# Kurtosis of 1024 rows: the last stage summed on TensorE with a factor row, other piece sizes, another split of x^4

## The chip, the cores and the metric

The kernel runs on one core of one Trainium2 chip. The metric is the device time of one execution in microseconds (us). A load moves data from HBM to SBUF; TensorE (PE) multiplies matrices into PSUM; VectorE (DVE), ScalarE (ACT) and GpSimd (POOL) work on tiles; SyncE (SP) issues the transfers.

## The reference

The input is 1024 rows of 8192 float32. Each row gives one number, its excess kurtosis:

```python
mean = np.mean(x, axis=-1, keepdims=True)
std = np.std(x, axis=-1, keepdims=True)
z = (x - mean) / (std + 1e-8)
return (np.mean(z ** 4, axis=-1) - 3).astype(np.float32)
```

With p2 and p4 the sums of the squared and fourth powers of x - mean, this is n p4 / p2^2 - 3, n = 8192 (the kernel leaves out the 1e-8).

## The kernel before

The rows are worked in 18 groups. A group takes 128/k rows, cut into k segments each, so that all 128 partitions are filled. Groups 0 and 1 have k = 8 (1024 columns a partition), group 2 has k = 4 (2048), groups 3 to 17 have k = 2 (4096 columns, 2 MB). `GROUPS` lists for each group k, the pieces in which its columns are loaded, how many columns of the fourth power ScalarE takes, and who sums for the mean. `load` issues one transfer per piece on SP's queue. The tiles lie in five slots (`SLOT_OF`), and `load_next` issues a group's loads, in order, when the group that held its slot is done.

The order of the work is written out by hand in the loop `for i in range(L)` (L = 17, the last group). Step i does this:

- `mean(i)`. For the first six groups VectorE adds the halves of the tile (`added_halves`, L149) and TensorE multiplies by a block matrix (L159). For 'PE' groups TensorE transposes the tile in chunks of 128 columns, adding them all up in `tps` (`transposed_sums`, L132); VectorE adds pairs of columns into `red` (`pair_sums`, L138), and a matmul with a column of -1/n gives minus the mean in `mps` (L168). The last group is of kind 'both': transposes for all but its last 512 columns, `added_halves` for these, two matmuls (L164, L165). ScalarE copies `mps` to `nmu` (L170).
- `square(i)`: ScalarE writes (x - mean)^2 over the tile and accumulates its sum in `s2` (L176).
- `fourth_dve(i - 1, ...)`: VectorE squares the previous group's tile again from some column on, and accumulates in `qd` (L188). Then `load_next(i - 1)`.
- a piece of the last stage of an earlier batch, if one is due in this step (`STEPS`).
- `fourth_act(i, ...)`: ScalarE does the same for the first columns, accumulating in `qa` (L183).

The groups are put into four batches for the last stage: groups 0 and 1, group 2, groups 3 to 12, groups 13 to 17. `finish(b)` is a generator in three parts, and `STEPS` says in which steps of the loop the parts of the first three batches are run: (7, 8, 9), (9, 10, 11) and (13, 14, 15). Its parts are `factor` (p2 = the segments' `s2` added up by a matmul, L204, and `fac` = -1/p2^2 by L206 and L208 on VectorE), `scaled` (`w4` = (qa + qd) times `fac`, L215 and L216) and `result` (a matmul into `pk` that adds up a row's segments and lays rows along the free axis, L226; minus 3, L228; the output transfer, L230).

The last group and the last batch are written out behind the loop. The last group's square is done in two halves of 2048 columns, the second half of the tile first, each with its own column of `s2`. VectorE does x^4 of columns 2048 to 4095 and of 1664 to 2047 (384 columns), and ScalarE of the first 1664. ScalarE multiplies its own sum by the factor (`wa`, L290), VectorE its own (L292), and two matmuls add `wa` and `w4` into one `pk`.

Of the kernel before, what the change touches and what calls it, by code (L numbers as in the profile page):

```python
# [7 lines left out]
f32 = mybir.dt.float32  # L8
bf16 = mybir.dt.bfloat16
AO = mybir.AluOpType  # L10
AF = mybir.ActivationFunctionType
P = 128
# [7 lines left out]
    (2, [4096], 1280, 'DVE'),  # L20
    (2, [4096], 768, 'DVE'),
    (2, [4096], 1536, 'DVE'),
    (2, [2304, 1792], 640, 'PE'),
    (2, [2304, 1792], 640, 'PE'),
    (2, [2304, 1792], 640, 'PE'),
    (2, [2304, 1792], 640, 'PE'),
    (2, [2304, 1792], 640, 'PE'),
    (2, [2304, 1792], 640, 'PE'),
    (2, [2304, 1792], 640, 'PE'),
    (2, [1536, 1536, 1024], 512, 'PE'),  # L30
    (2, [1536, 1536, 1024], 512, 'PE'),
    (2, [1536, 1536, 1024], 512, 'PE'),
    (2, [1536, 1536, 1024], 512, 'PE'),
    (2, [1536, 1280, 768, 512], 1664, 'both'),
]

BATCHES = [[0, 1], [2], [3, 4, 5, 6, 7, 8, 9, 10, 11, 12], [13, 14, 15, 16, 17]]
SLOT_W = 4096
SLOT_OF = [0, 1, 2, 3, 0, 1, 2, 3, 4, 0, 1, 2, 3, 4, 0, 1, 2, 3]
HALVES = 2  # L40


@with_exitstack
def kernel(
# [5 lines left out]
    nc = tc.nc  # L50
    n_rows, n_cols = x.shape
# [3 lines left out]
    L = NG - 1  # L55
    KS = [g[0] for g in GROUPS]
# [4 lines left out]
    const = ctx.enter_context(tc.tile_pool(name="const", bufs=1))  # L61
    small = ctx.enter_context(tc.tile_pool(name="small", bufs=4))
    fin = ctx.enter_context(tc.tile_pool(name="fin", bufs=4))
    psum = ctx.enter_context(tc.tile_pool(name="psum", bufs=2, space=bass.MemoryType.PSUM))
    psfin = ctx.enter_context(tc.tile_pool(name="psfin", bufs=1, space=bass.MemoryType.PSUM))
# [7 lines left out]
    blk = {}  # L73

    def block_matrix(k):
        r = P // k
        b = const.tile([P, P], f32, name=f"blk{k}")
        v = b.rearrange("p (r k) -> p r k", k=k)
        nc.gpsimd.memset(b, neg_inv_n)
        nc.gpsimd.affine_select(  # L80
            out=v, in_=v, pattern=[[-k, r], [0, k]], base=0,
            channel_multiplier=1, compare_op=AO.is_ge, fill=0.0)
        nc.gpsimd.affine_select(  # L83
            out=v, in_=v, pattern=[[k, r], [0, k]], base=k - 1,
            channel_multiplier=-1, compare_op=AO.is_ge, fill=0.0)
        blk[k] = b

    for k in dict.fromkeys(k for k in KS if k > 2):
# [4 lines left out]
        out=ident, in_=ident, pattern=[[-1, P]], base=0,  # L93
        channel_multiplier=1, compare_op=AO.is_equal, fill=0.0)
    negcol = const.tile([P, 1], f32, name="negcol")
    nc.gpsimd.memset(negcol, neg_inv_n)
    block_matrix(2)
    junk = const.tile([P, 2048], bf16, name="junk")

    where = {}
    stats = []
    for b in BATCHES:
        n = len(b) + (b[-1] == L)
        s2, qa, qd = (const.tile([P, n], f32, name=f"{t}_{b[0]}") for t in ("s2", "qa", "qd"))
        if any(GROUPS[i][2] == 0 for i in b):
            nc.gpsimd.memset(qa, 0.0)
        stats.append((s2, qa, qd))
        for j, i in enumerate(b):  # L110
            where[i] = (j, s2, qa, qd)

    slots = [xpool.tile([P, SLOT_W], f32, name=f"xt{s}") for s in sorted(set(SLOT_OF))]
    xts = {}
# [40 lines left out]
    def mean(i):  # L155
        k, pieces, _, engine = GROUPS[i]
        mps = psum.tile([P, 1], f32, name="mps")
        if engine == "DVE":
            nc.tensor.matmul(mps, lhsT=blk[k], rhs=added_halves(i, 0), start=True, stop=True)  # L159
        elif engine == "both":  # L160
            c = sum(pieces[:-1])
            tps = transposed_sums(i, c)
            part = added_halves(i, c)
            nc.tensor.matmul(mps, lhsT=pair_sums(tps), rhs=negcol, start=True, stop=False)  # L164
            nc.tensor.matmul(mps, lhsT=blk[k], rhs=part, start=False, stop=True)  # L165
        else:
            tps = transposed_sums(i, n_cols // k)
            nc.tensor.matmul(mps, lhsT=pair_sums(tps), rhs=negcol, start=True, stop=True)  # L168
        nmu = small.tile([P, 1], f32, name="nmu")
        nc.scalar.copy(nmu, mps)  # L170
        nmus[i] = nmu

    def square(i, c0=0, c1=None, extra=0):
        j, s2, qa, qd = where[i]
        t = xts[i][:, c0:c1]
        nc.scalar.activation(out=t, in_=t, func=AF.Square, bias=nmus[i],  # L176
                             accum_out=s2[:, j + extra:j + extra + 1])

    def fourth_act(i, c0, c1):
        j, s2, qa, qd = where[i]  # L180
        if c1 > c0:
            t = xts[i][:, c0:c1]
            nc.scalar.activation(out=t, in_=t, func=AF.Square, accum_out=qa[:, j:j + 1])  # L183

    def fourth_dve(i, c0, c1=None, extra=0):
        j, s2, qa, qd = where[i]
        t = xts[i][:, c0:c1]
        nc.vector.tensor_tensor_reduce(  # L188
            out=t, in0=t, in1=t, scale=1.0, scalar=0.0,
            op0=AO.mult, op1=AO.add, accum_out=qd[:, j + extra:j + extra + 1])  # L190

    def factor(b):
        s2 = stats[BATCHES.index(b)][0]
        n = len(b)
        k = KS[b[0]]
        p2 = psfin.tile([P, n], f32, name="p2")
        if b[-1] == L:
            nc.tensor.matmul(p2[:, :n - 1], lhsT=blk[k], rhs=s2[:, :n - 1], start=True, stop=True)  # L200
            nc.tensor.matmul(p2[:, n - 1:n], lhsT=blk[k], rhs=s2[:, n - 1:n], start=True, stop=False)  # L201
            nc.tensor.matmul(p2[:, n - 1:n], lhsT=blk[k], rhs=s2[:, n:n + 1], start=False, stop=True)
        else:
            nc.tensor.matmul(p2, lhsT=blk[k], rhs=s2, start=True, stop=True)  # L204
        rec = fin.tile([P, n], f32, name="rec")
        nc.vector.reciprocal(rec, p2)  # L206
        fac = fin.tile([P, n], f32, name="fac")
        nc.vector.scalar_tensor_tensor(  # L208
            out=fac, in0=rec, scalar=-1.0, in1=rec, op0=AO.mult, op1=AO.mult)
        return fac  # L210

    def scaled(b, fac, n):
        s2, qa, qd = stats[BATCHES.index(b)]
        w4 = fin.tile([P, len(b)], f32, name="w4")
        nc.vector.tensor_add(w4[:, :n], qa[:, :n], qd[:, :n])  # L215
        nc.vector.tensor_mul(w4[:, :n], w4[:, :n], fac[:, :n])  # L216
        return w4

    def result(b, terms):
        n = len(b)  # L220
        k = KS[b[0]]
        r = P // k
        sel = blk[k].rearrange("p (r k) -> p r k", k=k)[:, :, 0]
        pk = psfin.tile([n, r], f32, name="pk")
        for j, t in enumerate(terms):
            nc.tensor.matmul(pk, lhsT=t, rhs=sel, start=j == 0, stop=j == len(terms) - 1)  # L226
        kr = fin.tile([n, r], f32, name="kr")
        nc.vector.tensor_scalar_add(kr, pk, -3.0)  # L228
        dst = out[ROWS[b[0]]:ROWS[b[-1] + 1]].rearrange("(g r) -> g r", r=r)
        nc.sync.dma_start(out=dst, in_=kr)  # L230

    def finish(b):
        fac = factor(b)
        yield
        w4 = scaled(b, fac, len(b))
        yield
        result(b, [w4])


    held = {}  # L240
# [18 lines left out]
    for b, ats in zip(BATCHES[:-1], STEPS):  # L259
        f = finish(b)  # L260
        for at in ats:
            steps.setdefault(at, []).append(f)
    for i in range(L):
        warm_up(WARM.get(i, 0))
        mean(i)
        square(i)
        if i >= 1:
            fourth_dve(i - 1, GROUPS[i - 1][2])
            load_next(i - 1)
        for f in steps.get(i, ()):  # L270
            next(f, None)
        fourth_act(i, 0, GROUPS[i][2])


    k, _, a, _ = GROUPS[L]
    h = n_cols // k // 2
    b = BATCHES[-1]
    n = len(b)
    s2, qa, qd = stats[-1]
    mean(L)  # L280
    square(L, h, 2 * h)
    fourth_dve(L - 1, GROUPS[L - 1][2])
    square(L, 0, h, extra=1)
    fourth_dve(L, h, 2 * h)
    fourth_act(L, 0, a)
    fac = factor(b)
    w4 = scaled(b, fac, n - 1)
    wa = fin.tile([P, n], f32, name="wa")
    nc.gpsimd.memset(wa, 0.0)
    nc.scalar.activation(out=wa[:, n - 1:], in_=qa[:, n - 1:n], func=AF.Copy, scale=fac[:, n - 1:])  # L290
    fourth_dve(L, a, h, extra=1)
    nc.vector.scalar_tensor_tensor(  # L292
        out=w4[:, n - 1:], in0=qd[:, n:], scalar=qd[:, n - 1:n], in1=fac[:, n - 1:],
        op0=AO.add, op1=AO.mult)
    result(b, [wa, w4])


# [28 lines left out]
```

## Time and profile before

| | |
|---|---|
| median of 10 executions | 97.85 us (97.44 to 99.23) |
| the profiled execution | 97.63 us; its span, first to last instruction, 95.9 us |
| VectorE, ScalarE, TensorE busy | 76.0, 79.8, 60.7 us |
| TensorE weight loads busy | 51.5 us |
| read from HBM | 33.55 MB, 350 GB/s over the span |
| mean granted TensorE clock | 0.959 of full speed |
| ScalarE, square of a full group (L176) | 14 of 128x4096, 3722 ns each |
| VectorE, x^4 (L188) | 7 of 128x3456, 3752 ns; 4 of 128x3584, 3884 ns |
| ScalarE, x^4 (L183) | 7 of 128x640, 737 ns; 4 of 128x512, 630 ns |
| TensorE, transposes (L132) | 380 of 128x128 |

A profile comes from one execution. Busy time counts the instructions of an engine; matmul ends are modelled. In a line of instructions, the numbers are the start in us from the span's beginning, the duration in us, the engine, the source line, the operation, output and input by name, their shapes, and in brackets how long the engine stood idle before it and whose work ended that. In the rows of slices the span is cut into 40 equal parts of 2.4 us, and a digit is the busy share in tenths. An engine that waits for nothing of importance can still look busy, so the stages are read one by one.

### The profile page before, as it was taken

To read this page: it belongs to the slowest core of one execution; us is meant where nothing else is said; L and a number is where in the kernel's file an instruction comes from. 1 tells how busy PE (TensorE), PEld (TensorE's weight loads), DVE (VectorE), ACT (ScalarE), POOL (GpSimd) and SP (SyncE) were. 2 spreads that over 40 slices of the span, in tenths; PEclk is the share of its full clock that TensorE was granted. 3 is DMA by queue.
4 is the path that set the end of the run, shared out by engine and by line. 5 is a ranking of instruction groups with operands and counts; after the bars stand their busy time and mean duration, and the time that the engine had idled before them with its cause. 6 is when DMAs were issued, how large, how long until landed. Compare 5 with 4: busy or idle time off the path is not lost.

```text
span 95.9 us, 1280 instructions
## 1 busy us (share of the span) xinstructions
PE 60.7 (63%) x446; PEld 51.5 (54%) x446; DVE 76.0 (79%) x86; ACT 79.8 (83%) x89; POOL 4.6 (5%) x19
## 2 busy tenths in 40 slices
PE   0040200209999797968796979797978797961330
PEld 0040200205477787957695969696967686950310
DVE  2235909899997937989797979697989797999980
ACT  6055270799999999999999999999999899899960
POOL 6830000000000000000000000000000000000000
PEclk9999999999999999999999999999999999998555
DMA  2999999999999999999999999999999999600000
GB/s 39 400 347 430 437 430 437 437 430 382 383 423 416 424 433 427 419 422 423 422 416 419 427 402 419 406 421 410 424 408 415 408 419 404 254 5 0 0 0 4
DMA packets 5226, 33.63 MB, mean 351 GB/s; under 512 B 612, under 2 KB 612, under 8 KB 3812
## 3 DMA queue, kind: packets, MB, share of 16 engines
q1 hardware_dynamic: 5220, 33.56, 85.5%
q8 instruction: 3, 0.05, 0.2%
q14 instruction: 3, 0.02, 0.1%
HBM read 33.55 MB, written 0.00 MB: 350 GB/s over the span
## 4 chain that ended last, share of the span: by engine, by line
DMA 53%; DVE 21%; PE 11%; issue 6%; ACT 6%; SPq 0%; DVEq 0%
DMA xt<-in_x_dram 53%; DVE xt L188 14%; PE tps L132 8%; DVE junk L149 6%; ACT xt L176 5%; PE pk L226 1%; DVE red L138 1%; PE mps L168 1%; PE mps L159 1%; SPq L126 0%; ACT nmu L170 0%; ACT wa L290 0%; DVE qd L188 0%; DVE kr L228 0%; DVE fac L208 0%
## 5 line engine op out<-in xcount | busy, mean ns | idle before, releaser
L176 ACT ACTIVATE xt<-xt,nmu 128x4096 f32<-128x4096 f32 (+2 forms) x19 | 60.4, 3178 | 0.6
L188 DVE CUSTOM_DVE_ANT_0 xt<-xt 128x3456 f32<-128x3456 f32 (+7 forms) x19 | 58.8, 3100 | 2.2 <-ACT xt L176 1.0
L132 PE MATMUL tps<-ident,xt 128*128 128x128 f32 x380 | 45.8, 275 | 1.0 <-DMA xt<-in_x_dram 0.9
L132 PEld LDWEIGHTS tps<-ident,xt 128*128 128x128 f32 x380 | 41.4, 141 | 3.5 <-DMA xt<-in_x_dram 2.9
L149 DVE CUSTOM_DVE_ANT_0 junk<-xt 128x2048 bf16<-128x2048 f32 (+3 forms) x7 | 10.0, 1427 | 7.3 <-DMA xt<-in_x_dram 7.3
L159 PE MATMUL mps<-part,blk 128*128 128x1 f32 x12 | 3.1, 332 | 19.5 <-DVE part L149 19.5
L159 PEld LDWEIGHTS mps<-part,blk 128*128 128x128 f32 x12 | 2.8, 290 | 20.6 <-issue 9.5
L183 ACT ACTIVATE xt<-xt 128x640 f32<-128x640 f32 (+5 forms) x15 | 12.9, 859 | 0.5
L170 ACT COPY nmu<-mps 128x1 f32<-128x1 f32 x18 | 2.7, 150 | 11.0 <-PE mps L159 10.1
L138 DVE TENSOR_REDUCE red<-tps 128x128 f32<-128x256 f32 x12 | 5.1, 423 | 6.7 <-PE tps L132 6.7
L168 PE MATMUL mps<-negcol,red 128*128 128x1 f32 x22 | 3.9, 247 | 6.6 <-DVE red L138 5.4
L168 PEld LDWEIGHTS mps<-negcol,red 128*128 128x128 f32 x22 | 3.3, 188 | 8.9 <-ACT xt L176 6.5
L256 PE MATMUL warm<-zeros 128*128 128x512 f32 x6 | 5.0, 996 | 0.0
L176 ACT ACTIVATION_READ_ACCUMULATOR xt<-xt,nmu 128x1 f32 x19 | 3.5, 184 | 0.0
L256 PEld LDWEIGHTS warm<-zeros 128*128 128x128 f32 x6 | 1.9, 336 | 2.1 <-issue 2.1
L183 ACT ACTIVATION_READ_ACCUMULATOR xt<-xt 128x1 f32 x15 | 2.8, 187 | 0.0
L201 PE MATMUL p<-s,blk 128*128 128x1 f32 x2 | 0.6, 363 | 2.2 <-ACT xt L176 2.2
L70 ACT ACT_TABLE_LOAD x1 | 1.3, 1283 | 0.8 <-PEq L310 0.8
L201 PEld LDWEIGHTS p<-s,blk 128*128 128x128 f32 x2 | 0.5, 312 | 2.2 <-ACT xt L176 2.2
L83 POOL TENSOR_SCALAR_AFFINE_SELECT blk<-blk 128x128 f32<-128x128 f32 x3 | 1.7, 563 | 0.2
L80 POOL TENSOR_SCALAR_AFFINE_SELECT blk<-blk 128x128 f32<-128x128 f32 x3 | 1.7, 553 | 0.2
L188 DVE DVE_READ_ACCUMULATOR2_ANT qd<- 128x1 f32 x19 | 1.6, 82 | 0.0
(34 smaller groups left out, 14.1 us busy)
## 6 DMA issues: line engine op xcount, KB each, us to landing
xt<-in_x_dram SPq DMA_DIRECT2D x7, 1152.0 KB, 11.5
xt<-in_x_dram SPq DMA_DIRECT2D x9, 768.0 KB, 11.6
xt<-in_x_dram SPq DMA_DIRECT2D x7, 896.0 KB, 13.1
xt<-in_x_dram SPq DMA_DIRECT2D x3, 2048.0 KB, 12.1
xt<-in_x_dram SPq DMA_DIRECT2D x6, 512.0 KB, 11.3
xt<-in_x_dram SPq DMA_DIRECT2D x1, 1024.0 KB, 7.6
xt<-in_x_dram SPq DMA_DIRECT2D x1, 640.0 KB, 11.6
xt<-in_x_dram SPq DMA_DIRECT2D x1, 384.0 KB, 10.7
```

The source lines that it names most:

```text
L80: nc.gpsimd.affine_select(out=v, in_=v, pattern=[[-k, r], [0, k]], base=0, channel_multiplier=1, compare_op=AO.is_ge, fill=0.0)
L83: nc.gpsimd.affine_select(out=v, in_=v, pattern=[[k, r], [0, k]], base=k - 1, channel_multiplier=-1, compare_op=AO.is_ge, fill=0.0)
L132: nc.tensor.matmul(tps, lhsT=xts[i][:, c:c + P], rhs=ident, start=c == 0, stop=c == w - P, is_transpose=True)
L138: nc.vector.tensor_reduce(out=red.rearrange("p (r k) -> p r k", k=2), in_=tps.rearrange("p (r k) -> p r k", k=2).unsqueeze(2).to_broadcast ...
L149: nc.vector.tensor_tensor_reduce(out=junk[:, :h], in0=t[:, :h], in1=t[:, h:], scale=1.0, scalar=0.0, op0=AO.add, op1=AO.add, accum_out=part)
L159: nc.tensor.matmul(mps, lhsT=blk[k], rhs=added_halves(i, 0), start=True, stop=True)
L168: nc.tensor.matmul(mps, lhsT=pair_sums(tps), rhs=negcol, start=True, stop=True)
L170: nc.scalar.copy(nmu, mps)
L176: nc.scalar.activation(out=t, in_=t, func=AF.Square, bias=nmus[i], accum_out=s2[:, j + extra:j + extra + 1])
L183: nc.scalar.activation(out=t, in_=t, func=AF.Square, accum_out=qa[:, j:j + 1])
L188: nc.vector.tensor_tensor_reduce(out=t, in0=t, in1=t, scale=1.0, scalar=0.0, op0=AO.mult, op1=AO.add, accum_out=qd[:, j + extra:j + extra ...
L256: nc.tensor.matmul(warm, lhsT=zeros[:, :P], rhs=zeros, start=True, stop=True)
```

## The change

Sums of fourth powers are no longer multiplied by the factor before the matmul. Instead -1/n times (p4 + a multiple of p2^2) is built up in `pk` on TensorE: one matmul with the squares of p2 (made on ScalarE, from PSUM) against a selection matrix scaled by -3n/k (`sel3`, made on POOL at the start), and one matmul for each of the tiles that hold sums of fourth powers (`quads`; the last batch has three of them). The factor goes through a matmul of its own into `pf`, ScalarE copies that to a row `frow` in SBUF, and VectorE multiplies `pk` by `frow`.

In the three parts of `finish` this stands as follows: p2, its square on ScalarE, reciprocal and factor; then the matmuls of the factor and of the squares and the copy of the factor row; then the matmuls of the fourth powers, the product and the output. The last batch now uses the same generator: its first part stands before `fourth_act(L, ...)`, its second between that and the last `fourth_dve`, its third at the end.

In `GROUPS`, groups 13 to 15 are loaded in two pieces where there were three. ScalarE takes 384 columns of the fourth power in groups 6 to 15 (640 in groups 6 to 12 and 512 in 13 to 15 before), 256 in group 16 (512 before), and 1536 in group 17 (1664 before). Group 17's mean is of kind 'PE' (32 transposes, no 'both').

```diff
-    (2, [2304, 1792], 640, 'PE'),
...
-    (2, [1536, 1536, 1024], 512, 'PE'),
-    (2, [1536, 1280, 768, 512], 1664, 'both'),
+    (2, [2304, 1792], 384, 'PE'),
...
+    (2, [1536, 1536, 1024], 256, 'PE'),
+    (2, [1536, 1280, 768, 512], 1536, 'PE'),
...
+    sel3 = {}
+    for k, b in blk.items():
+        sel3[k] = const.tile([P, P // k], f32, name=f"sel3_{k}")
+        nc.gpsimd.tensor_scalar_mul(
+            sel3[k], b.rearrange("p (r k) -> p r k", k=k)[:, :, 0], -3.0 * n_cols / k)
...
+        quads = [const.tile([P, n], f32, name=f"q{t}_{b[0]}") for t in range(2 + last)]
...
+    def finish(b):
...
+        sq = fin.tile([P, n], f32, name="sq")
+        nc.scalar.activation(out=sq, in_=p2, func=AF.Square)
         rec = fin.tile([P, n], f32, name="rec")
         nc.vector.reciprocal(rec, p2)
         fac = fin.tile([P, n], f32, name="fac")
         nc.vector.scalar_tensor_tensor(
             out=fac, in0=rec, scalar=-1.0, in1=rec, op0=AO.mult, op1=AO.mult)
-        return fac
-
-    def scaled(b, fac, n):
-        s2, qa, qd = stats[BATCHES.index(b)]
-        w4 = fin.tile([P, len(b)], f32, name="w4")
-        nc.vector.tensor_add(w4[:, :n], qa[:, :n], qd[:, :n])
-        nc.vector.tensor_mul(w4[:, :n], w4[:, :n], fac[:, :n])
-        return w4
...
+        yield
+        pf = psfin.tile([n, r], f32, name="pf")
         pk = psfin.tile([n, r], f32, name="pk")
-        for j, t in enumerate(terms):
-            nc.tensor.matmul(pk, lhsT=t, rhs=sel, start=j == 0, stop=j == len(terms) - 1)
+        nc.tensor.matmul(pf, lhsT=fac, rhs=sel, start=True, stop=True)
+        nc.tensor.matmul(pk, lhsT=sq, rhs=sel3[k], start=True, stop=False)
+        frow = fin.tile([n, r], f32, name="frow")
+        nc.scalar.activation(out=frow, in_=pf, func=AF.Copy, scale=-float(n_cols) / k)
+        yield
+        for q in quads:
+            nc.tensor.matmul(pk, lhsT=q, rhs=sel, start=False, stop=q is quads[-1])
         kr = fin.tile([n, r], f32, name="kr")
-        nc.vector.tensor_scalar_add(kr, pk, -3.0)
+        nc.vector.tensor_mul(kr, pk, frow)
...
+    f = finish(BATCHES[-1])
     mean(L)
     square(L, h, 2 * h)
     fourth_dve(L - 1, GROUPS[L - 1][2])
-    square(L, 0, h, extra=1)
+    square(L, 0, h, second=1)
     fourth_dve(L, h, 2 * h)
+    next(f)
     fourth_act(L, 0, a)
-    fac = factor(b)
-    w4 = scaled(b, fac, n - 1)
-    wa = fin.tile([P, n], f32, name="wa")
-    nc.gpsimd.memset(wa, 0.0)
-    nc.scalar.activation(out=wa[:, n - 1:], in_=qa[:, n - 1:n], func=AF.Copy, scale=fac[:, n - 1:])
-    fourth_dve(L, a, h, extra=1)
-    nc.vector.scalar_tensor_tensor(
-        out=w4[:, n - 1:], in0=qd[:, n:], scalar=qd[:, n - 1:n], in1=fac[:, n - 1:],
-        op0=AO.add, op1=AO.mult)
-    result(b, [wa, w4])
+    next(f)
+    fourth_dve(L, a, h, second=1)
+    next(f, None)
```

## The prediction

> **What bounds the kernel now.** I read the slices of the span first (busy tenths, granted TensorE clock, DMA), then the chain that ended last, then the timeline of one middle group and of the tail.
>
> ```profile
> DVE  2235909899997937989797979697989797999980
> ACT  6055270799999999999999999999999899899960
> ...
> PEclk9999999999999999999999999999999999998555
> DMA  2999999999999999999999999999999999600000
> ```
>
> Here the DMA engines are full from slice 1 to slice 33, about 82 us, and ScalarE is nearly full for as long. The last 11 us have no load in them: that tail belongs to VectorE, ScalarE and TensorE. So the time is a stretch at the pace of the loads plus a tail, and the chain's shares say the same: more than half is loads, and what is left is spread over all three engines.
>
> ```profile
> DMA 53%; DVE 21%; PE 11%; issue 6%; ACT 6%; SPq 0%; DVEq 0%
> ```
>
> To find the pace I took each load's last arrival from the trace. Groups loaded in two pieces (2304 + 1792 columns: groups 7, 8, 10, 11, 12) end 4.965 us apart on average. Groups in three or four pieces (13 to 17) end 5.04 us apart; the three one-piece groups 3 to 5 are 4.90 us apart. The last load of group 17 lands at 84.61. The engines' cycles in a middle group, from the timeline:
>
> ```profile
> 61.23 0.42 DVE L138 TENSOR_REDUCE red<-tps 128x128 f32<-128x256 f32 x1 [0.77 <-PE tps L132]
> 61.26 0.74 ACT L183 ACTIVATE xt<-xt 128x640 f32<-128x640 f32 x1
> 61.58 3.75 DVE L188 CUSTOM_DVE_ANT_0 xt<-xt 128x3456 f32<-128x3456 f32 x1
> ...
> 61.81 0.35 PE L168 MATMUL mps<-negcol,red 128*128 128x1 f32 x2 [0.61 <-DVE red L138]
> ...
> 62.02 3.69 PE L132 MATMUL tps<-ident,xt 128*128 128x128 f32 x32
> ...
> 62.39 3.74 ACT L176 ACTIVATE xt<-xt,nmu 128x4096 f32<-128x4096 f32 x1
> ```
>
> TensorE needs 3.73 us from its first transpose to the pair reduction, 0.58 to the mean's matmul and 0.21 to the next transposes: about 4.66 us when nothing is late (57.36 to 62.02), less than the loads' 4.965. ScalarE's own work is 3.74 + 0.74 + two accumulator reads + the copy, 4.96 less small overlaps. VectorE needs 0.35 + 3.75 + 0.08, about 4.2. Loads and ScalarE are thus level, and the transposes' starts follow landings. The tail:
>
> ```profile
> 85.78 3.89 DVE L188 CUSTOM_DVE_ANT_0 xt<-xt 128x3584 f32<-128x3584 f32 x1
> ...
> 86.65 2.00 ACT L176 ACTIVATE xt<-xt,nmu 128x2048 f32<-128x2048 f32 x1
> ...
> 88.65 1.99 ACT L176 ACTIVATE xt<-xt,nmu 128x2048 f32<-128x2048 f32 x1
> ...
> 90.76 1.59 ACT L183 ACTIVATE xt<-xt 128x1664 f32<-128x1664 f32 x1
> 90.78 0.59 PE L202 MATMUL p<-s,blk 128*128 128x1 f32 x2 [1.40 <-ACT xt L176]
> ...
> 92.38 0.55 DVE L188 CUSTOM_DVE_ANT_0 xt<-xt 128x384 f32<-128x384 f32 x1
> ...
> 92.53 0.29 ACT L290 ACTIVATE wa<-qa,fac 128x1 f32<-128x1 f32 x1
> ...
> 92.97 0.22 DVE L292 SCALAR_TENSOR_TENSOR w<-qd,fac 128x1 f32<-128x1 f32 x1
> ...
> 93.25 0.38 PE L226 MATMUL pk<-blk,w 128*5 128x64 f32 x2
> 93.66 0.21 DVE L228 TENSOR_SCALAR kr<-pk 5x64 f32<-5x64 f32 x1 [0.47 <-PE pk L226]
> ```
>
> VectorE (last x^4 piece done at 92.94) and ScalarE (wa done at 92.82) end together. ScalarE goes straight from the second half-square into its x^4 piece, while p2 is summed beside it (90.78 to 91.37).
>
> **What the Trainium skill says.** "ScalarE: Activation LUTs", What ACT_TABLE_LOAD costs: an ACTIVATE with immediates takes 186 ns + 0.833 ns a column, a pointer operand adds some 93, and neighbours overlap by about 93. The trace agrees: 630 ns for 512 columns (612 by the rule), 3722 for 4096 with a pointer bias (3692). "TensorE: Matmul & The Clock Gate", Engine queue depths: ScalarE and VectorE take their instructions strictly in order. No row shows otherwise, and it makes a wait in front of ScalarE's x^4 piece count in full. The same page, Part 1: an idle array falls back to half clock; the slices show it, 0.5 in the last three.
>
> **The change, part by part.** Times are of the profiled execution: span 95.9 us, 97.63 us in all (1.73 outside the span). The median shown is 97.85, 0.22 above it.
>
> **1. Column shares in the loop.** Groups 6 to 12 take 256 columns from ScalarE, 13 to 15 take 128, 16 takes 256: 2432 x 0.84 ns (from 737 against 630 ns for 640 and 512) = 2.04 us off ScalarE. VectorE gains the same columns at 1.03 ns (3884 against 3752 for 3584 and 3456): +0.26 us a group, making 4.45. The loads at 4.965 cover VectorE, and they cover ScalarE's gain too: nothing moves. If that cover were gone, this would be -0.21 us a group. Slots come free 0.26 us later, but loads are issued some 11.5 us before they land and queue behind others: zero.
>
> **2. Earlier batches' last stage.** Each adds a square and a copy on ScalarE (by the page 0.19 to 0.24 us, 0.10 to 0.15 beyond the overlap; six in all, 0.75 us), takes two small VectorE operations of 0.16 off, and puts three more matmul pairs on TensorE at some 0.25 us each: two in one step (8, 10, 14), one in the next (9, 11, 15). ScalarE has 0.2 us a group freed. TensorE's cycle is 4.66 + 0.5 = 5.16 in a two-pair step, 0.2 over the loads, made up in the next. The pair of the squares waits for ScalarE, with the next transposes queued behind it: in step 14 the square follows ScalarE's work of 70.96 and is done at about 71.17, when the mean's matmul is; in step 8 some 0.2 late (41.8 against 41.59), but the next transposes wait for a landing at 44.50. In steps 14 and 15 little room is left, counted under 3. POOL gains three small multiplies at the start; their results are first used after 40 us.
>
> **3. Two pieces for groups 13 to 15.** Loads gain 3 x (5.04 - 4.965) = 0.22 us: group 15 lands at 74.31, not 74.54. SP issues three loads fewer (0.33 each, far ahead of need), and its output transfers keep their places. But 14 transposes then wait for the last piece in place of 8. Group 15's reduction comes at 74.31 + 0.05 + 1.75 = 76.11 (75.74 before). With 0.58 to the mean and 0.7 through two pairs of q, group 16's transposes start at 77.4 (76.81). Before, they stopped for a landing at 78.30; now everything needed is there in time and they run 3.73 us: reduction at 81.13 (80.78). Group 17, all 32 transposes now on TensorE (its 512-column VectorE sum, 0.42 us, and a second mean matmul, 0.22, go): start 81.13 + 0.79 = 81.92, reduction 85.66 (85.28). Then 0.58 to the mean, 0.39 to the copy, 0.19 to the square: **ScalarE's first half-square starts at 86.82, against 86.65: +0.17**. The landing gain is lost.
>
> **4. ScalarE's tail.** In the changed order the square of p2 stands before ScalarE's last x^4 piece. It waits for p2: from the second half-square's accumulator (86.82 + 4.07) 0.06 + 0.59 + 0.02, then about 0.19 itself. So x^4 starts 4.95 us after the first half-square, not 4.11: +0.84. It has 1536 columns, not 1664: -0.09; with its accumulator it ends at +6.55, so **93.37**. The copy of the factor row follows, under the matmuls.
>
> **5. VectorE's tail.** x^4 of group 16 waits for that group's square, started about 0.34 late like its mean: 86.12. It has 256 more columns (+0.26), two small operations go (-0.27), the last piece is 512 not 384 (+0.13): it ends near **93.5**. The following 0.28 us operation is gone.
>
> **6. The sums on TensorE.** Three pairs (q0, q1, q2) stand in order behind ScalarE's end: 0.04 + 0.38 for the first and about 0.18 each for two more (two matmuls started 0.09 apart at half clock, from L226), where one pair of 0.39 stood. Then 0.02 + 0.21 for the product. q2 is ready by then. End: 86.82 + 6.59 + 0.74 + 0.23 = 94.38 against 93.87, **+0.5 us**. The sum: +0.17 (start) +0.84 - 0.09 (ScalarE) and, in place of what ran from 92.45 to 93.87 (1.42), now 1.01 after ScalarE's end: +0.51.
>
> **Unknown prices.** The squares and copies on tiny PSUM tiles: 0.15 (the copy of L170) to 0.29 (L290); I take 0.19; up to 0.1 us on the path. Back-to-back small pairs: 0.1 to 0.38 each, so -0.15 to +0.4. The landing interval of groups 13 to 15: 4.90 to 5.04, so -0.2 to +0.2, and less than nothing only if the landing is what counts. The POOL multiplies lie between 0.1 us (its memset) and 0.8 each, and nobody waits for them.
>
> **Rivals.**
> *The loads set the end and their gain carries through.* If groups 13 to 15 come at the one-piece interval, 0.43 us is gained; if in addition ScalarE's wait is short, so that VectorE ends last, its path is worth -0.03 by itself (4.07 + 2.22 + 0.42 + 0.68 + 0.67 against 8.09). That gives 97.63 - 0.46 = 97.2, or 97.4 in the median: faster. It decides from 4.93 us a group on and needs TensorE not to fall behind. For it: the full DMA row. Against: the 14 late transposes, and p2's fixed 0.59.
> *The wait is covered.* Landings, not TensorE's cycle, pace group 16 (start -0.2 rather than +0.17), with the tail's +0.34 kept: 97.8, median 98.0, no change.
> *VectorE becomes the loop's bound.* At 4.45 plus up to 0.45 of last-stage operations it comes within 0.1 us of the loads. If the added matmuls push the reductions behind x^4, four steps lose some 0.15: 98.7, median 98.95.
>
> **How the numbers follow.** A measurement of this kernel tells about 0.5% (0.49 us) from no change. Forecast, +0.5 in the profile, rounded up with the loop's risk: 98.45 in the median, its own range 98.0 to 98.9, chance 0.58. Loads carry: 0.14. Covered: 0.18. VectorE bound: 0.10. The forecast's own range straddles the limit of 98.34; with most of it above and all of the third rival, slower has 0.58, no change 0.30, faster 0.12. The range reaches from the faster rival's upper part to the third rival's far end: 97.6 to 99.2.
>
> **What would show it.** Right: the last group of ScalarE shows an idle of 0.6 to 0.7 before the square of p2; its x^4 ends later than before by some 0.9; three pairs at the end, the first released by ScalarE; group 16's transposes without a landing wait; no change in the middle's 4.97 a group. Wrong: groups under 4.9 us apart in the middle, or a chain through VectorE in the last 3 us, or the second half of group 15 landing well before 74.2.

## The result, and the profile after

The changed kernel takes **99.18 us** in the median of 15 executions (98.39 to 100.93), the kernel before 97.79 in the same comparison: a ratio of **1.0119** (95% interval 1.0092 to 1.0146), about 1.16 us slower. The direction is the forecast one, the size is about twice the forecast. The medians are over all executions and the ratio leaves out those that ran in a slower state, so comparisons below go by the ratio.

The profiled execution took 99.63 us, 0.45 above the median; its span is 97.9. Its slices, as before (VectorE, ScalarE, granted TensorE clock, DMA):

```profile
DVE  1339459899996739795597979799979798999960
ACT  6064712999999999989297999899979999999760
PEclk9999999999999999985999999999999999999655
DMA  1999999999999999999999999999999997000000
```

The loads end as early as before (the last lands at about 84.3 us, before at 84.6). New, counting slices from 0, are dips of VectorE in slices 18 and 19 and of ScalarE in slice 19, and a dip of the array's clock in slices 17 and 18. The chain that ended last has changed its nature:

```profile
PE 33%; ACT 31%; DMA 13%; DVE 12%; issue 8%; DVEq 0%
```

Loads were 53% of it and are 13%: from about 18 us on no load is in it any more, it runs through the engines. The waits, summed over the run (engine, line, whom it waited for; us in total, times, longest), name a new one:

```profile
ACT nmu L178 <- PE mps L176: 4.9, 8, 1.9
...
DVE rec L219 <- ACT sq L217: 1.7, 3, 0.6
...
PEld tps L140 <- DMA xt<-in_x_dram: 0.5, 2, 0.3
```

VectorE's reciprocal waits for ScalarE's square of p2, three times 0.56 us. The transposes' weight loads waited 2.9 us for loads before, now 0.5: TensorE is behind its data. The timeline of the first of these places, steps 7 to 9 of the changed kernel:

```profile
36.28 3.84 PE L140 MATMUL tps<-ident,xt 128*128 128x128 f32 x32
...
36.92 3.72 ACT L184 ACTIVATE xt<-xt,nmu 128x4096 f32<-128x4096 f32 x1
...
40.63 0.15 ACT L217 ACTIVATE sq<-p 128x2 f32<-128x2 f32 x1
...
40.81 0.17 DVE L219 RECIPROCAL rec<-p 128x2 f32<-128x2 f32 x1 [0.56 <-ACT sq L217]
...
41.09 0.42 DVE L146 TENSOR_REDUCE red<-tps 128x128 f32<-128x256 f32 x1
...
41.66 0.35 PE L176 MATMUL mps<-negcol,red 128*128 128x1 f32 x2 [1.53 <-DVE red L146]
...
42.32 5.35 PE L140 MATMUL tps<-ident,xt 128*128 128x128 f32 x32
```

The square of p2 stands on ScalarE behind a whole group's square (36.92 to 40.6). In the program both the square and the reciprocal read `p2`, the square comes first, and the reciprocal is made to wait for it. Behind the reciprocal, in VectorE's order, stands the pair reduction of the next group. Its transposes ended at 40.12; it comes at 41.09, 0.97 late. Of this, 0.56 is the wait; the rest is VectorE's own x^4 of the group before, which ended at 40.25, and the reciprocal and the factor. In the other two places, steps 10 and 14, the reduction comes 0.34 (52.99 after 52.65) and 0.72 us (72.67 after 71.95) behind its transposes, with the same wait of 0.56 in front of it. TensorE, which waits for the reduction, stood idle for 1.53 us here, and the next 32 transposes took 5.35 us, not 3.7. A table by stage shows the clock at which it ran (stretch; its length; busy us and instructions of TensorE, its weight loads, VectorE, ScalarE, GpSimd; granted clock; DMA share; GB/s):

```profile
40.00:42.00 2.00, 0.47 (x7) 0.36 (x5) 1.41 (x6) 1.37 (x5) 0.00 (x0) 1.00 0.99 410
42.00:44.00 2.00, 1.89 (x18) 1.80 (x18) 2.00 (x1) 1.92 (x2) 0.00 (x0) 0.86 1.04 438
44.00:46.00 2.00, 2.00 (x12) 2.00 (x11) 1.45 (x2) 2.00 (x3) 0.00 (x0) 0.50 0.99 412
```

After the stretch in which TensorE was busy for 0.47 of 2 us, the array ran at half clock, from 43.45 to 46.86. In this first place the late reduction itself cost almost nothing: by the trace the first piece of group 9 landed at 42.18, and its transposes began at 42.32. The 1.65 us come from the clock. In steps 10 and 14 it is the other way round: the clock is full, and the next group's first piece had landed (52.12, 71.99) well before the late reduction let its transposes start (54.10, 73.77). The tail of the changed kernel:

```profile
87.38 4.16 DVE L196 CUSTOM_DVE_ANT_0 xt<-xt 128x3840 f32<-128x3840 f32 x1
...
88.06 2.00 ACT L184 ACTIVATE xt<-xt,nmu 128x2048 f32<-128x2048 f32 x1
...
92.81 0.18 ACT L217 ACTIVATE sq<-p 128x5 f32<-128x5 f32 x1 [0.67 <-PE p L212]
92.88 1.48 ACT L191 ACTIVATE xt<-xt 128x1536 f32<-128x1536 f32 x1
...
93.98 0.69 DVE L196 CUSTOM_DVE_ANT_0 xt<-xt 128x512 f32<-128x512 f32 x1
...
94.12 0.38 PE L226 MATMUL pf<-blk,fac 128*5 128x64 f32 x2 [1.35 <-DVE fac L221]
...
94.51 0.85 PE L232 MATMUL pk<-blk,q 128*5 128x64 f32 x6
...
95.46 0.21 DVE L234 TENSOR_TENSOR kr<-pk,frow 5x64 f32<-5x64 f32 x1 [0.78 <-PE pk L232]
```

So this execution is 2.0 us above the one before in three parts. The last group's first half-square starts at 88.06, not 86.65: +1.41. From there to the end of the last VectorE operation it takes 7.61 us, not 7.22: +0.39. The rest of the span, with the output transfer, takes 0.2 more.

### The profile page after: what moved, and what is told of

Same layout as the page of the kernel before. It is cut to its first block, busy times and chain, and to the rows that moved or that the text cites. A ratio compares the mean times of both kernels' runs of the same rounds, so it can differ in the third digit from the quotient of the medians.

```text
span 97.9 us, 1323 instructions
## 1 busy us (share of the span) xinstructions
PE 62.8 (64%) x472; PEld 55.1 (56%) x472; DVE 77.3 (79%) x75; ACT 78.3 (80%) x96; POOL 6.0 (6%) x22
## 4 chain that ended last, share of the span: by engine, by line
PE 33%; ACT 31%; DMA 13%; DVE 12%; issue 8%; DVEq 0%
ACT xt L184 28%; PE tps L140 20%; DMA xt<-in_x_dram 13%; PE warm L255 5%; DVE red L146 4%; DVE xt L196 3%; DVE junk L157 3%; PE mps L176 3%; ACT xt L191 1%; PE pk L232 1%; PE mps L167 1%; ACT nmu L178 1%; PE pf L226 1%; DVE rec L219 1%; PE pk L227 0%
## 5 line engine op out<-in xcount | busy, mean ns | idle before, releaser
L196 DVE CUSTOM_DVE_ANT_0 xt<-xt 128x3712 f32<-128x3712 f32 (+7 forms) x19 | 61.5, 3240 | 2.0 <-ACT nmu L178 1.0
L140 PE MATMUL tps<-ident,xt 128*128 128x128 f32 x384 | 46.4, 280 | 0.2
L140 PEld LDWEIGHTS tps<-ident,xt 128*128 128x128 f32 x384 | 43.8, 145 | 1.1 <-DMA xt<-in_x_dram 0.5
L157 DVE CUSTOM_DVE_ANT_0 junk<-xt 128x2048 bf16<-128x2048 f32 (+2 forms) x6 | 9.7, 1614 | 6.0 <-DMA xt<-in_x_dram 6.0
L191 ACT ACTIVATE xt<-xt 128x384 f32<-128x384 f32 (+4 forms) x15 | 10.7, 715 | 0.3
L176 PE MATMUL mps<-negcol,red 128*128 128x1 f32 x24 | 4.4, 251 | 8.8 <-DVE red L146 7.0
L219 DVE RECIPROCAL rec<-p 128x2 f32<-128x2 f32 (+3 forms) x4 | 0.7, 186 | 1.7 <-ACT sq L217 1.7
L226 PE MATMUL pf<-blk,fac 128*2 128x16 f32 (+3 forms) x8 | 1.2, 233 | 1.4 <-DVE fac L221 1.4
L232 PE MATMUL pk<-blk,q 128*5 128x64 f32 (+3 forms) x18 | 1.9, 247 | 0.0
```

Of the source, the lines that this page charges most:

```text
L140: nc.tensor.matmul(tps, lhsT=xts[i][:, c:c + P], rhs=ident, start=c == 0, stop=c == w - P, is_transpose=True)
L157: nc.vector.tensor_tensor_reduce(out=junk[:, :h], in0=t[:, :h], in1=t[:, h:], scale=1.0, scalar=0.0, op0=AO.add, op1=AO.add, accum_out=part)
L196: nc.vector.tensor_tensor_reduce(out=t, in0=t, in1=t, scale=1.0, scalar=0.0, op0=AO.mult, op1=AO.add, accum_out=quads[1 + second][:, j:j + 1])
L226: nc.tensor.matmul(pf, lhsT=fac, rhs=sel, start=True, stop=True)
L232: nc.tensor.matmul(pk, lhsT=q, rhs=sel, start=False, stop=q is quads[-1])
```

## The experiments

Two more quantities from the profiles are used below: the start of the last group's first half-square ("start") and the time from there to the end of VectorE's last operation ("tail"). A single profiled execution carries chance of its own: in each of them some landings come late (last section), so starts are compared with care, while the tail lies behind the loads.

| kernel | median us | before, same chip | ratio to before (95%) | start | tail |
|---|---|---|---|---|---|
| before | 97.79 | | 1 | 86.65 | 7.22 |
| changed | 99.18 | 97.79 | 1.0119 (1.0092 to 1.0146) | 88.06 | 7.61 |
| rec_first_loop | 98.55 | 97.91 | 1.0052 (1.0026 to 1.0079) | 86.81 | 7.65 |
| stage_only | 99.90 | 97.91 | 1.0160 (1.0113 to 1.0208) | 88.51 | 7.67 |
| groups_only | 98.54 | 97.91 | 1.0073 (1.0041 to 1.0105) | 87.80 | 7.82 |
| tail_square_late | 99.40 | 97.91 | 1.0130 (1.0085 to 1.0175) | 87.82 | 7.61 |
| before_plus_square | 98.70 | 98.04 | 1.0035 (1.0006 to 1.0064) | 86.96 | 7.22 |
| sums_reordered | 98.52 | 98.04 | 1.0042 (1.0013 to 1.0070) | 86.68 | 7.37 |
| pieces_back | 98.38 | 98.04 | 1.0052 (1.0027 to 1.0076) | 86.78 | 7.57 |
| all_mends | 98.11 | 98.04 | 1.0007 (0.9969 to 1.0046) | 87.80 | 7.25 |
| array_kept_busy | 98.91 | 97.86 | 1.0103 (1.0043 to 1.0162) | 87.54 | 7.64 |

**rec_first_loop: the reciprocal first.**

```diff
         sq = fin.tile([P, n], f32, name="sq")
-        nc.scalar.activation(out=sq, in_=p2, func=AF.Square)
+        if b[-1] == L:
+            nc.scalar.activation(out=sq, in_=p2, func=AF.Square)
         rec = fin.tile([P, n], f32, name="rec")
...
             out=fac, in0=rec, scalar=-1.0, in1=rec, op0=AO.mult, op1=AO.mult)
+        if b[-1] != L:
+            nc.scalar.activation(out=sq, in_=p2, func=AF.Square)
```

> Only the order of two readers of p2 is changed, in the three batches inside the loop: VectorE's reciprocal stands ahead of ScalarE's square in the program, so it waits for the matmul alone, and the square waits for it. Theory A (in steps 7, 9 and 13 the reciprocal waits for the square, which stands behind a full group's square on ScalarE, and holds up the pair reduction queued behind it): the 0.56 us idles before the reciprocal go, the reductions of groups 8, 10 and 14 come when their transposes end, and the time falls by 0.6 to 0.9 us, to 98.3 to 98.6 with before at 97.8. Rival B (the extra matmul pairs on TensorE and the two-piece loads put the transposes behind, as the prediction had it): 99.1, no change against the changed kernel.

The ratio falls from 1.0119 to 1.0052, and the intervals do not meet: 0.67%, 0.65 us (give or take some 0.4), is the price of the order of two readers, whatever it does to the clock included. No instruction is added or removed. In its timeline the reciprocal of step 7 has no wait:

```profile
40.59 0.17 DVE L220 RECIPROCAL rec<-p 128x2 f32<-128x2 f32 x1
40.79 0.16 DVE L222 SCALAR_TENSOR_TENSOR fac<-rec 128x2 f32<-128x2 f32 x1
40.87 0.42 DVE L146 TENSOR_REDUCE red<-tps 128x128 f32<-128x256 f32 x1
...
42.45 3.83 PE L140 MATMUL tps<-ident,xt 128*128 128x128 f32 x32 [0.47 <-DMA xt<-in_x_dram]
```

The reduction still comes 0.75 us behind its transposes (these ended at 40.12), as VectorE's x^4 ended at 40.67; but group 9's transposes wait for a landing again and run at full clock.

The two profiles show where the time goes. Group 9's transposes start no earlier than in the changed kernel (42.45 against 42.32); they end earlier, by the clock alone. Group 11's start 1.68 us earlier (52.42 against 54.10), group 14's 0.82 (67.44 against 68.26), group 15's 1.34 (72.43 against 73.77). So the changed kernel made up half of its first loss in steps 11 to 13, and the third late reduction, in step 14, opened it again.

The half clock is not needed for a loss. tail_square_late and array_kept_busy (below) keep the three waits and have no half clock in the loop in their profiles. There group 14's transposes start at landings again (68.11 after 67.97, 67.84 after 67.71), so the first two places are made up; the third puts group 15's transposes 0.59 and 0.58 us behind their landing (73.53 after 72.94, 73.25 after 72.67), against 0.16 here (72.43 after 72.27). That is 0.4 us of the 0.65, in single profiles.

**before_plus_square: the square alone, in the kernel before.**

```diff
+        if b[-1] != L:
+            sq = fin.tile([P, n], f32, name="sq")
+            nc.scalar.activation(out=sq, in_=p2, func=AF.Square)
         rec = fin.tile([P, n], f32, name="rec")
```

> The kernel before, with one addition: in the three batches inside the loop ScalarE squares p2 ahead of VectorE's reciprocal in the program, as the changed kernel does; nobody uses the square. Theory A (the reciprocal's wait for that square is what slows the loop): about 0.56 to 1.0 us of idle before each of the three reciprocals, and 0.5 to 0.9 us more in all, 98.4 to 98.8 with before at 97.9. Rival (three small squares on ScalarE cost only their own 0.15 us, and the cost needs the extra matmul pairs): 97.9 to 98.1.

By the ratio the kernel is 0.35% slower, 0.34 us, with an interval from 0.06 to 0.63 us. That lies between theory A's range and the rival's and reaches into both. The waits are there, even longer, since ScalarE's x^4 has 640 columns here:

```profile
DVE rec L209 <- ACT sq L207: 3.0, 3, 1.0
```

So three unused squares of 0.15 us each slow the kernel, and in the profile the three reductions come 1.01, 0.39 and 0.70 us behind their transposes. The time alone does not tell this wait from the squares' own 0.45 us. If they cost less here than in the changed kernel (the intervals do not settle it), that would fit the wait of the transposes for loads, 2.3 us in this profile against 0.5: TensorE still catches up.

**stage_only: the new last stage, the old groups.** The change is the old `GROUPS` list in the changed kernel.

> The new last stage with the old list of groups (640/512/1664 columns on ScalarE, three pieces for groups 13 to 15, the last mean by both engines). Theory A: the wait for the square stays, and each square on ScalarE ends later with 640 columns, so the cost stays or grows: 98.9 to 99.4. Rival B: without the late second pieces the transposes keep up, and only the tail costs: 98.1 to 98.3. A third view, that the column shares are what costs: 97.8.

At 1.0160, some 99.5 by the ratio, it is the slowest of all, at the upper end of theory A's range, and rival B is out: the new stage makes the larger part of the cost. Whether 640 columns on ScalarE make it larger than in the changed kernel is not shown, as the intervals overlap (six executions). The reciprocals wait longer, because the squares come later:

```profile
DVE rec L219 <- ACT sq L217: 2.9, 3, 1.0
```

This profile too has a stretch at half clock in group 9's transposes (last section). And with 1664 columns ScalarE's last x^4 is what the final sums wait for, the link that the prediction's step 6 had:

```profile
95.06 0.80 PE L232 MATMUL pk<-blk,q 128*5 128x64 f32 x6 [0.35 <-ACT xt L191]
```

**groups_only: the old last stage, the new groups.** The change is the new `GROUPS` list in the kernel before.

> The old last stage with the new list of groups. Theory A: no wait is added; the loads gain some 0.2, and ScalarE's and VectorE's shares are covered by the loads: 97.6 to 98.0. Rival B: the two-piece loads alone delay group 16's transposes by 0.2 to 0.35 us: 98.0 to 98.3. Third view (column shares cost): 98.8 or more.

All three expectations failed: 1.0073, at 98.54 between theory B and the third view. The tail, 0.60 us longer, holds most of it:

```profile
87.12 4.16 DVE L188 CUSTOM_DVE_ANT_0 xt<-xt 128x3840 f32<-128x3840 f32 x1
...
87.80 2.00 ACT L176 ACTIVATE xt<-xt,nmu 128x2048 f32<-128x2048 f32 x1
...
94.00 0.68 DVE L188 CUSTOM_DVE_ANT_0 xt<-xt 128x512 f32<-128x512 f32 x1
...
94.72 0.22 DVE L292 SCALAR_TENSOR_TENSOR w<-qd,fac 128x1 f32<-128x1 f32 x1
...
95.41 0.21 DVE L228 TENSOR_SCALAR kr<-pk 5x64 f32<-5x64 f32 x1 [0.47 <-PE pk L226]
```

VectorE's last pieces grew from 3.89 and 0.55 us to 4.16 and 0.68, the first of them starts 0.68 us ahead of the half-square where it was 0.87, nothing was taken off VectorE behind them, and the tail is 7.82 instead of 7.22. (The late start, 87.80, holds late landings: group 9's transposes waited 1.54 us for one at 43.41.) In the loop the shares cost nothing visible: its pair reductions from group 9 to group 15 come every 4.95 to 5.04 us, the pace of the loads. The two halves of the change do not add up (1.60% and 0.73% against 1.19%). A likely reason, not tested: the new stage takes three small operations off VectorE's tail, and the new groups bring the squares earlier (waits of 0.56 us, not 1.0).

**tail_square_late: ScalarE's x^4 first in the tail.**

```diff
+        if b[-1] == L:
+            fourth_act(L, 0, GROUPS[L][2])
+            nc.scalar.activation(out=sq, in_=p2, func=AF.Square)
...
     next(f)
-    fourth_act(L, 0, a)
     next(f)
```

(These three lines stand behind the factor, in place of the square ahead of the reciprocal.)

> Only the tail is changed against the changed kernel: the last batch's reciprocal is ahead of the square of p2 in the program, and ScalarE's square of p2 stands behind its last x^4 piece, so this piece starts right after the second half-square. The prediction's step 4 says that ScalarE's x^4 then ends 0.84 us earlier; VectorE's 512 columns end last, and the three sums on TensorE wait for it: 0.3 us less than the changed kernel, 98.8. If the wait for p2 in front of ScalarE's piece were free, no change: 99.1. In the loop nothing changes.

The first expectation failed: no change, as its alternative had it. ScalarE's piece starts 0.7 us earlier against the half-square (4.11 us behind it, not 4.82) and ends at 93.51, yet the tail is 7.61 as before the edit, and the ratio is no better.

```profile
91.93 1.48 ACT L191 ACTIVATE xt<-xt 128x1536 f32<-128x1536 f32 x1
...
93.66 0.17 DVE L222 SCALAR_TENSOR_TENSOR fac<-rec 128x5 f32<-128x5 f32 x1
...
93.88 0.38 PE L230 MATMUL pf<-blk,fac 128*5 128x64 f32 x2 [1.35 <-DVE fac L222]
94.06 0.41 PE L231 MATMUL pk<-sel,sq 128*5 128x64 f32 x2
94.27 0.84 PE L236 MATMUL pk<-blk,q 128*5 128x64 f32 x6
```

The end does not hang on ScalarE. It hangs on VectorE's factor: TensorE's five pairs stand in order, the factor's pair first, and from its start at 93.88 to the end of the last sum at 95.11 they take 1.2 us, although the input of the second half's sum had been there since 93.5.

**sums_reordered: the pairs in the order of their inputs.** This is rec_first_loop with, in the last batch:

```diff
+        late = quads
+        if b[-1] == L:
+            nc.tensor.matmul(pk, lhsT=sq, rhs=sel3[k], start=True, stop=False)
+            nc.tensor.matmul(pk, lhsT=quads[1], rhs=sel, start=False, stop=False)
+            nc.tensor.matmul(pf, lhsT=fac, rhs=sel, start=True, stop=True)
+            late = [quads[0], quads[2]]
...
-        for q in quads:
+        for q in late:
```

> The kernel with the reciprocal first in the loop (98.55), with only the order of the last batch's small matmuls changed: squares, second half's x^4, then the factor row, then ScalarE's x^4 and the last 512 columns, where the factor row came first. Theory C (the end is VectorE's factor and then five matmul pairs in a row, 94.25 - 92.91 = 1.34 us): only one pair follows the last x^4, and the end comes 0.3 us earlier, 98.2 to 98.3. Rival, as the prediction's step 6 had it (the three sums wait for ScalarE's x^4, which ends at about the same time as the factor): two pairs still follow, 0.1 us or less, 98.45.

In the profile the tail is 7.37 instead of 7.65, 0.28 us less, as theory C has it (0.3):

```profile
92.74 0.38 PE L233 MATMUL pf<-blk,fac 128*5 128x64 f32 x2
93.13 0.60 PE L242 MATMUL pk<-blk,q 128*5 128x64 f32 x4
...
93.84 0.21 DVE L244 TENSOR_TENSOR kr<-pk,frow 5x64 f32<-5x64 f32 x1 [0.54 <-PE pk L242]
```

The times cannot tell it: 1.0042 against 1.0052, with intervals that overlap widely. The profile shows the mechanism; its worth in the median stays open.

**pieces_back: three pieces for groups 13 to 15.** This is rec_first_loop with `[1536, 1536, 1024]` for these groups.

> The kernel with the reciprocal first in the loop (98.55), with groups 13 to 15 loaded in three pieces again. The prediction's step 3 (two pieces delay group 16's transposes by 0.35 us and the first half-square by 0.17): the half-square of the last group starts about 0.15 us earlier and group 16's transposes wait for a landing again; 98.4. Rival (two pieces are worth their 0.22 us of earlier landings): 98.75.

Neither: the ratio is 1.0052, to the digit that of rec_first_loop, and the last half-square starts at 86.78 against 86.81. Group 16's reduction is 0.27 earlier (80.87 against 81.14), but group 17 then waits for its own loads, which land 0.17 later (84.70 against 84.53). The piece sizes make no difference that shows.

**all_mends: everything that was found, together.** The reciprocals first everywhere, ScalarE's last x^4 before its square and 1792 columns long (256 left to VectorE), three pieces for groups 13 to 15, and this order of the last batch's sums:

```diff
+            nc.tensor.matmul(pk, lhsT=quads[1], rhs=sel, start=True, stop=False)
+            nc.tensor.matmul(pf, lhsT=fac, rhs=sel, start=True, stop=True)
+            nc.tensor.matmul(pk, lhsT=quads[0], rhs=sel, start=False, stop=False)
+            nc.tensor.matmul(pk, lhsT=sq, rhs=sel3[k], start=False, stop=False)
+            late = [quads[2]]
```

> The changed kernel with reciprocals first everywhere, ScalarE's last x^4 ahead of its square of p2 and 1792 columns long (VectorE's last piece 256), the last batch's sums in the order in which their inputs come, and groups 13 to 15 in three pieces. If the three costs found so far are all there is (wait in the loop, order of the sums, VectorE's longer tail), the end comes about 0.15 us ahead of the kernel before: 97.7 to 97.9 with before at 97.9. If something else in the change costs too, 98.2 or more.

1.0007 (0.9969 to 1.0046): within 0.5% the new last stage with these mends costs nothing, and gains nothing either. The time lies between its two expectations. Its tail is 7.25, about that of the kernel before, not 0.15 shorter as expected. So these changes together take the loss away; apart from the reciprocal's order, which of them does how much is not shown. No version here beats the kernel before.

**array_kept_busy: a dummy matmul in TensorE's gaps.**

```diff
             tps = transposed_sums(i, n_cols // k)
+            if i in (8, 10, 14):
+                warm_up(1)
```

> The changed kernel with one dummy matmul (128x512 on zeros, some 0.9 us, result unused) on TensorE between the transposes and the mean's matmul of groups 8, 10 and 14, the places where TensorE waits 0.9 to 1.5 us for the late pair reduction. The wait itself stays. Theory D (the idle of 1.53 us in step 8 lets the array's clock fall to half in part of the executions, and group 9's transposes then take 5.35 us, not 3.7): no execution shows such a stretch, and the median falls from 99.2 to 98.8 or 98.9, the time of executions without it. Rival (the clock falls for a reason of its own, or the late reduction alone is the cost): no change, or up to 0.2 us more for dummies that end late.

The median of 98.91 is in theory D's range, but the ratio does not bear it out: 1.0103 (1.0043 to 1.0162) against the changed kernel's 1.0119, no difference that shows. In its profile the reciprocals still wait, group 8's dummy fills the gap, and group 9's transposes take their usual time:

```profile
40.78 1.02 PE L257 MATMUL warm<-zeros 128*128 128x512 f32 x2
...
41.63 0.17 DVE L221 RECIPROCAL rec<-p 128x2 f32<-128x2 f32 x1 [0.56 <-ACT sq L219]
...
42.95 3.71 PE L140 MATMUL tps<-ident,xt 128*128 128x128 f32 x32
```

But two kernels without the dummy, before_plus_square and tail_square_late, also ran these transposes at full clock after idles of 1.57 and 1.72 us. So neither what the clock takes from the median nor that the dummy holds it is shown.

## Why the prediction was right or wrong

The forecast was slower, +0.5 us in the profile and 98.45 in the median, in its own range of 98.0 to 98.9; it came out about 1.16 us slower, 99.18. Right in the direction, half the size. With the loop's wait taken out (rec_first_loop) the loss is 0.51 us by the ratio, close to what the forecast had counted; the other half is a wait that it did not count. That 99.18 still lies in its wider range (to 99.2) is luck: that end belongs to a rival that did not happen.

- **Step 1 (column shares in the loop cost nothing):** right. The loop of groups_only keeps the pace of the loads, and rec_first_loop, with the new shares, starts its tail at 86.81 against 86.65.
- **Step 2 (the earlier batches' last stage costs nothing beside the loads): this is the step that failed.** It counted the square's duration (0.19 taken, 0.15 measured) and asked who on TensorE waits for it. It did not ask whether the reciprocal, the other reader of p2, is made to wait for it. The square's place, behind a whole group's square on ScalarE, and the reduction's place, behind the reciprocal on VectorE, turned 0.15 us of work into three waits of 0.56 us ahead of reductions that TensorE needs next. rec_first_loop prices it at 0.65 us. The text looked at step 8 (the pair "some 0.2 late") and let it go, because a landing covered it. In the profile a landing did cover the late reduction there, but not the half clock that followed (group 9's reduction at 47.71, before 46.33); and in steps 10 and 14 there was no landing to cover it. TensorE's cycle was also taken too long: its terms add up to 4.52, not 4.66, which holds a short wait for a landing, and the changed kernel runs it in 4.53 (58.98 to 63.51).
- **Step 3 (start of the tail +0.17):** without the late reductions the number is met: group 16's reduction at 81.14 (81.13 forecast), group 17's at 85.66 (85.66), the half-square at 86.81 (86.82). Its cause is not confirmed: pieces_back undoes the two pieces, which brings group 16's reduction 0.27 forward (0.35 by the forecast), and still starts at 86.78.
- **Step 4 (ScalarE's wait for p2):** met. The idle is 0.67 us; the x^4 starts 4.82 us behind the half-square (4.95 forecast) and ends at +6.38 (6.55). The Trainium skill's strict order on ScalarE ("TensorE: Matmul & The Clock Gate", Engine queue depths) is seen here: x^4 had its input and stood behind the square.
- **Steps 5 and 6 (the three sums wait for ScalarE):** the tail is +0.39 where +0.34 was forecast, but the last link is another one. VectorE's factor and five pairs behind it end the kernel; ScalarE's x^4 may come 0.7 us earlier without effect (tail_square_late). The sum hid this, as both ends were nearly level: it treated the factor's pair and the squares' pair as done in waiting time. That the size fits is in part luck.
- **The rivals:** the loads did not carry their gain through, and the wait was not covered. VectorE as the loop's bound, 98.95, is nearest in size but not what happened: VectorE stood idle, waiting.
- **The signs named in advance:** the idle before the last square and group 16's transposes without a landing wait came true; the unchanged middle and a first pair released by ScalarE did not. Two signs of being wrong came true: the chain's last 3 us run through VectorE (91.55 to 94.08) before the sums, and some groups in the middle are under 4.9 us apart (the reductions at 57.85, 62.73 and 67.25), here because TensorE was catching up, not because the loads were faster.

## What to carry to other kernels

When an operation is added, look not only at what it takes but at who else reads or writes its tiles: a second reader that is placed first in the program can become a wait for the first, and everything queued behind that reader inherits it. Put the reader with critical work behind it first, and let small matmuls stand in the order in which their inputs arrive. In a loop where loads and engines are level, a gap of a microsecond is made up slowly (here 1.68 us shrank to 0.82 in three groups), and near the end not at all.

## What the runs showed that was not expected

- Half clock in the middle of the run. In the changed kernel and in stage_only the array's granted clock fell to 0.50 after idles of 1.53 and 1.58 us, for 3.41 us in both, and 32 transposes took 5.35 us instead of 3.7 to 3.85. An idle of 1.72 us at the same place of tail_square_late was not followed by a fall, nor was one of 1.57 us in before_plus_square. So the length of the idle alone does not decide it; what does was not tried. From stage_only, then tail_square_late:

```profile
41.61 0.35 PE L176 MATMUL mps<-negcol,red 128*128 128x1 f32 x2 [1.58 <-ACT xt L191]
...
42.35 5.35 PE L140 MATMUL tps<-ident,xt 128*128 128x128 f32 x32 [0.20 <-DMA xt<-in_x_dram]
...
42.37 0.35 PE L176 MATMUL mps<-negcol,red 128*128 128x1 f32 x2 [1.72 <-DVE red L146]
...
43.29 3.84 PE L140 MATMUL tps<-ident,xt 128*128 128x128 f32 x32 [0.38 <-DMA xt<-in_x_dram]
```

- Late landings. In the trace a load lands with sixteen arrivals. From some point on, one or a few of the sixteen come later than the others and stay behind. In the changed kernel fifteen arrivals of group 9's first piece came at 41.12, at the usual distance of 2.79 us from the load before, and the last at 42.18; in rec_first_loop they came at 41.10 and 42.31. The loads as a whole did not pause: the table above has the DMA share at 0.99 and 410 GB/s from 40 to 42 us. How many arrivals are late and by how much differs between executions (up to some 1.5 us); the cause was not looked into. It is one reason why starts of single profiles differ by up to a microsecond.
